# The output gate of a hybrid decoder layer: 64 column loads become 8 whole-row loads and one sum

## The chip, the cores and the metric

The kernel runs on one core of one Trainium2 chip. A core has five engines that run side by side and meet through semaphores: PE (TensorE, matrix products), DVE (VectorE), ACT (ScalarE), POOL (GpSimd) and SP (SyncE), which issues nearly all of this kernel's transfers. Each engine takes its instructions in order. The metric is the time of one execution on the device, in microseconds (us), as the median of the runs; lower is better.

## The reference, cut to what matters

One decoder layer on 1024 tokens of width 1024, all in float32. A conditioning vector `c` gives shift, scale and gate through one product; the gate is the last third of it and scales the layer's contribution to the residual stream at the very end.

```python
mod = c @ w_ada[l] + b_ada[l]                      # (1, 3072)
shift, scale, gate = jnp.split(mod, 3, axis=-1)
h = rmsnorm(x, norm_gain[l]) * (1.0 + scale[:, None, :]) + shift[:, None, :]
proj = h @ w_in[l]                                 # q, k, v, gates of both branches
...
o_a = stick_breaking_attention(...)                # 8 heads of 64
...
o_b = latent_attention(...)                        # 8 heads
...
merged = jax.nn.sigmoid(g_a) * y_a + jax.nn.sigmoid(g_b) * y_b
x = x + gate[:, None, :] * (merged @ w_out[l])
return rmsnorm(x, final_norm_gain)
```

So the gate is a vector of 1024 numbers, a product of `c` (1024) with a 1024x1024 slice of `w_ada`, needed only in the last tenth of the kernel.

## The kernel before, in words

The opening stage loads x and weights, makes h transposed (`hh` and `hl`, a rounded part and the rest, since products are made of three passes of rounded operands), and the first q, k and v. Then four pairs of stick-breaking heads follow (`sb_pair(m)`, m = 0 to 3). For each head and each of 8 query blocks i, `sb_scores` makes scores with q and k on PE (L723, L724, into `ps_s`), two sigmoids on ACT (`surv`, `beta`), a running product on DVE (the scan, L727) and the weights on POOL (L729, L730, `beta`). `finish` then turns the weights with PE (L678, into `ps_t`), takes them out as `wth` (ACT) and `wtl` (the rest, DVE), and multiplies them with v (L695, into `ps_o`) after every second block.

Beside a pair runs `filler`, a generator of projection jobs. One job loads a 512 KB column block of `w_in` (`raw`, issued by SP), splits it into `whi` (DVE) and `wlo` (mostly POOL), and makes two halves of 24 matmuls of 512 columns each (L298, into `ps_g`). The halves are taken out through `ev`, a buffer of two slots, by ACT, or as q and k of the next pair by ACT and DVE (`q1a`, `kl1b` and the like). POOL also works off a chain of small operations for the rotary tables (`rope`, tiles `rp`).

The third generator, `gates_gen`, computes the output gate. Before the change, `gate_part(n)` works on 128 of the 1024 columns at a time: for k = 0 to 7 it loads a 128x128 block of `w_ada` into `wg`, which takes a slot of `ev`, and adds block times `c` to `ga` on DVE (L794, L796). It then loads the bias (L799, L800), rounds the sum into `gr` (two tiles), sums the 128 rows with two matmuls against `ones_r` (L807), copies the row out (DVE) and stores it to `gate_d`. The loop around the pairs advances it by one step in each step of pairs 0, 1 and 2.

The order on each engine isn't that of the code. A scheduler reorders the instructions by a timeline of its own, within what the tiles' slots and data allow, so that gate steps, scans, casts and evacuations are mixed on DVE, and `wg`, `raw`, `v` and the stores on SP.

Of the kernel before, what the change touches and what calls it, by code (L numbers as in the profile page):

```python
# [10 lines left out]
F32 = mybir.dt.float32  # L11
F32R = mybir.dt.float32r
# [3 lines left out]
ALU = mybir.AluOpType  # L16
# [3 lines left out]
P = 128  # L20
S = 1024
D = 1024
NT = S // P
KD = D // P
# [19 lines left out]
def hsl(hf):  # L44
    return slice(hf * 512, (hf + 1) * 512)
# [3 lines left out]
def hybrid_layer(ctx: ExitStack, tc: tile.TileContext, x, c, positions, w_ada, b_ada, norm_gain, w_in,  # L49
                 q_norm_gain, w_uq, kv_norm_gain, w_ukv, w_branch_a, w_branch_b, w_out, final_norm_gain, out):  # L50
    nc = tc.nc
    xf, of = x[0], out[0]
    win = w_in[0].rearrange("(k p) n -> p k n", p=P)
    wada = w_ada[0].rearrange("(k p) n -> p k n", p=P)
# [18 lines left out]
    def ps_tile(tag):  # L73
        return PS["pool"].tile([P, 512], F32, tag=tag, name="ps_" + tag, bufs=PS["bufs"][tag])
# [5 lines left out]
    gate_d = dram.tile([1, D], F32, name="gate_d")  # L80
# [3 lines left out]
    def copy(eng, o, i):  # L84
        if eng == "a":
            nc.scalar.activation(o, i, AF.Copy)  # L86
        elif eng == "v":
            nc.vector.tensor_copy(out=o, in_=i)  # L88
        else:
            nc.gpsimd.tensor_scalar(out=o, in0=i, scalar1=1.0, scalar2=None, op0=ALU.mult)  # L90

    def rd(t):
        return t.bitcast(F32)

    def rest(eng, o, full, hi):
        (nc.vector if eng == "v" else nc.gpsimd).tensor_tensor(out=o, in0=full, in1=rd(hi), op=ALU.subtract)  # L96
# [219 lines left out]
    def advance(gen, n):  # L316
        for _ in range(n):
            if next(gen, "end") == "end":
                return False
        return True  # L320
# [42 lines left out]
    def load_v(m):  # L363
        st = pairs[m]
        st.v = sbp.tile([P, NT, 2, P], F32R, name=f"v{m}", tag="v", bufs=2)
        nc.sync.dma_start(out=rd(st.v), in_=v_d[:, :, m])
# [50 lines left out]
    with tc.tile_pool(name="start", bufs=1, **RW, side="right") as st:  # L417
# [167 lines left out]
        for k in range(KD):  # L585
            n = k + 1
# [74 lines left out]
    evp = evx.enter_context(tc.tile_pool(name="evp", bufs=2, **RW, side="right"))  # L661
    sbx = ExitStack()
    sbp = sbx.enter_context(tc.tile_pool(name="sbp", bufs=1, **RW, side="right"))
# [69 lines left out]
    def sb_pair(m):  # L733
        st = pairs[m]
        og = sbp.tile([P, S], F32, name=f"oga{m}", tag="og", bufs=1)
        todo = []
        for h in range(2):
            wts = {}
            for i in range(NT):
                beta = sb_scores(m, h, i)  # L740
                todo.append((h, i, beta))
                yield
                if len(todo) > 1:
                    finish(m, st, og, todo.pop(0))
                    yield
        finish(m, st, og, todo.pop(0))
        yield
        nc.sync.dma_start(out=oa_d[m], in_=og)
# [34 lines left out]
    ones_r = base.tile([P, 1], F32R, name="ones_r")  # L783
    nc.vector.tensor_copy(out=ones_r, in_=ones_c)

    def gate_part(n):
        c0 = 2 * D + n * 128
        ga = sbp.tile([P, 128], F32, name="ga", tag="ga", bufs=1)
        for k in range(KD):
            wg = evp.tile([P, 512], F32, name="wg", tag="ev")[:, 0:128]  # L790
            nc.sync.dma_start(out=wg, in_=wada[:, k, c0:c0 + 128])
            cc = col[:, R_C + k:R_C + k + 1]
            if k == 0:
                nc.vector.tensor_scalar(out=ga, in0=wg, scalar1=cc, scalar2=None, op0=ALU.mult)  # L794
            else:
                nc.vector.scalar_tensor_tensor(out=ga, in0=wg, scalar=cc, in1=ga, op0=ALU.mult, op1=ALU.add)  # L796
            yield
        wg = evp.tile([P, 512], F32, name="wg", tag="ev")[0:1, 0:128]
        nc.sync.dma_start(out=wg, in_=b_ada[:, c0:c0 + 128])  # L799
        nc.vector.tensor_tensor(out=ga[0:1], in0=ga[0:1], in1=wg, op=ALU.add)  # L800
        yield
        gr = [sbp.tile([P, 128], F32R, name=f"gr{i}", tag=f"gr{i}", bufs=1) for i in range(2)]
        copy("v", gr[0], ga)
        rest("v", gr[1], ga, gr[0])
        ps = ps_tile("g")
        for i in range(2):
            nc.tensor.matmul(out=ps[0:1, 0:128], lhsT=ones_r, rhs=gr[i], start=i == 0, stop=i == 1)  # L807
        wg = evp.tile([P, 512], F32, name="wg", tag="ev")[0:1, 0:128]
        copy("v", wg, ps[0:1, 0:128])
        nc.sync.dma_start(out=gate_d[:, n * 128:(n + 1) * 128], in_=wg)  # L810
        yield

    gates_gen = itertools.chain.from_iterable(gate_part(n) for n in range(8))
    for m in range(NPAIR):
        units = 14 if m + 1 < NPAIR else 16 - TAILF
        done = 0
        for step, _ in enumerate(sb_pair(m)):
            want = min(units, units * (step + 1) // 31)
            advance(filler, want - done)
            done = want  # L820
            if m in (1, 2):
                advance(rope, 2)
            if step == VLS and m + 1 < NPAIR:
                load_v(m + 1)
            if m < 3:
                advance(gates_gen, 1)
        advance(filler, units - done)
    advance(rope, 1000)
# [28 lines left out]
    with tc.tile_pool(name="latw", bufs=2, **RW, side="right") as lp:  # L857
# [32 lines left out]
        for t in range(NT):  # L890
# [4 lines left out]
            for k in range(KD):  # L895
                for n, (m, w) in enumerate(((hh, wch), (hh, wcl), (hl, wch))):
# [7 lines left out]
            v = small.tile([P, 2], F32, name="vl", tag="vl")  # L904
# [7 lines left out]
                                    op0=ALU.mult)  # L912
# [77 lines left out]
    for k in range(2):  # L990
        raw = up.tile([P, S], F32, name="ur", tag="ur", bufs=URB)
        nc.sync.dma_start(out=raw, in_=wukv[:, k, :])
        g = col[:, R_KG + k:R_KG + k + 1]
# [64 lines left out]
    for t in range(NT):  # L1058
        tsl = slice(t * P, (t + 1) * P)
        pq = [ps_tile("g"), ps_tile("s")]  # L1060
        for k in range(3):
            for n, (m, w) in enumerate(((cq_h, wqh), (cq_h, wql), (cq_l, wqh))):
                for b in range(2):
                    nc.tensor.matmul(out=pq[b][:, 0:384], lhsT=m[:, k, tsl], rhs=w[:, k, b * 384:(b + 1) * 384],  # L1064
                                     start=k == 0 and n == 0, stop=k == 2 and n == 2)
# [16 lines left out]
        if t > 3:  # L1082
            b, n = divmod(t - 4, 2)
# [148 lines left out]
    step, done, total = 0, 0, 2 * len(yajobs) - len(UQF) - UQE  # L1232
# [64 lines left out]
    for t in range(NT):  # L1297
# [8 lines left out]
        for n, (hf, c0, wc) in enumerate(parts):  # L1306
            hi, lo = wos[hf]
            cs, gs = slice(c0, c0 + wc), slice(hf * 512 + c0, hf * 512 + c0 + wc)
            ps = ps_tile("sgt"[n])
            for k in range(KD):  # L1310
                for i, (m, w) in enumerate(((mg[0], hi), (mg[0], lo), (mg[1], hi))):
                    nc.tensor.matmul(out=ps[:, 0:wc], lhsT=m[k][:, tsl], rhs=w[:, k, cs],  # L1312
                                     start=k == 0 and i == 0, stop=k == KD - 1 and i == 2)
# [5 lines left out]
            if n == 0:  # L1319
                nc.vector.tensor_scalar(out=acc, in0=ss[:, 0:1], scalar1=1.0 / D, scalar2=EPS, op0=ALU.mult,  # L1320
                                        op1=ALU.add)
            else:
                nc.vector.scalar_tensor_tensor(out=acc, in0=ss[:, n:n + 1], scalar=1.0 / D, in1=acc, op0=ALU.mult,
                                               op1=ALU.add)
# [31 lines left out]
```

## Time and profile before

| | |
|---|---|
| median of 3 runs | 1001.03 us (1000.28 to 1006.5) |
| profiled execution | 1001.96 us |
| its span, first to last instruction | 1000.2 us |
| busy in the span | PE 954.9 us (95%), DVE 647.6 (65%), ACT 435.5 (44%), POOL 388.5 (39%) |
| mean granted clock of PE | 0.992 of 2.4 GHz |
| gate work | from 121.9 us (first load) to 403.0 us (last store) |

A profile's busy time counts an engine as busy while an instruction is under way. Matmuls overlap, so the duration of one (0.39 us for 512 columns) is longer than the distance to the next; the distances between starts are the ones to add up. "Idle before, releaser" is the time an engine stood before an instruction, and what ended that.

### The profile page before, as it was taken

To read this page: it belongs to the slowest core of one execution; us is meant where nothing else is said; L and a number is where in the kernel's file an instruction comes from. 1 tells how busy PE (TensorE), PEld (TensorE's weight loads), DVE (VectorE), ACT (ScalarE), POOL (GpSimd) and SP (SyncE) were. 2 spreads that over 40 slices of the span, in tenths; PEclk is the share of its full clock that TensorE was granted. 3 is DMA by queue.
4 is the path that set the end of the run, shared out by engine and by line. 5 is a ranking of instruction groups with operands and counts; after the bars stand their busy time and mean duration, and the time that the engine had idled before them with its cause. 6 is when DMAs were issued, how large, how long until landed. Compare 5 with 4: busy or idle time off the path is not lost.

```text
span 1000.2 us, 14638 instructions
## 1 busy us (share of the span) xinstructions
PE 954.9 (95%) x5100; PEld 815.5 (82%) x5100; DVE 647.6 (65%) x1294; ACT 435.5 (44%) x981; POOL 388.5 (39%) x393
## 2 busy tenths in 40 slices
PE   4979998998999989999999999999999999999997
PEld 3657877887787878888888999988899998877886
DVE  4862566678568857476655454774689997586544
ACT  4363433343333443343443432543488886333211
POOL 1100399994434435345444000621103332586322
PEclk9989999999999999999999999999999999999999
DMA  9733452213322142212122500479555332884322
GB/s 292 226 114 106 150 164 76 82 35 82 117 87 77 39 141 71 65 43 85 56 82 71 156 17 1 158 261 307 186 137 148 102 96 80 269 263 157 126 85 85
DMA packets 127140, 122.40 MB, mean 122 GB/s; under 512 B 16029, under 2 KB 97050, under 8 KB 126682
## 3 DMA queue, kind: packets, MB, share of 16 engines
q1 hardware_dynamic: 127002, 121.45, 39.2%
q8 instruction: 40, 0.66, 0.3%
q14 instruction: 34, 0.28, 0.1%
q10 hardware_dynamic: 64, 0.02, 0.0%
HBM read 86.80 MB, written 34.64 MB: 121 GB/s over the span
## 4 chain that ended last, share of the span: by engine, by line
PE 74%; DVE 10%; DMA 9%; issue 3%; ACT 2%; POOL 1%; SPq 1%; DVEq 0%; POOLq 0%; ACTq 0%
PE ps_g L298 29%; PE ps_o L695 6%; PE ps_t L678 6%; PE ps_g L1312 4%; PE ps_s L1312 4%; DMA wg<-in_w_ada 4%; PE ps_g L898 3%; PE ps_s L899 3%; PE ps_s L1133 2%; PE ps_s L1135 2%; PE ps_s L1134 2%; PE ps_t L1013 2%; DVE acc L483 1%; PE ps_s L533 1%; PE ps_g L1064 1%
## 5 line engine op out<-in xcount | busy, mean ns | idle before, releaser
L298 PE MATMUL ps_g<-hh,whi 128*128 128x512 f32 x448 | 179.3, 400 | 1.5 <-DVE kl1b L96 1.5
L298 PE MATMUL ps_g<-hl,whi 128*128 128x512 f32 x448 | 177.3, 396 | 0.0
L298 PE MATMUL ps_g<-hh,wlo 128*128 128x512 f32 x448 | 176.8, 395 | 0.0
L96 POOL TENSOR_TENSOR wlo<-raw,whi 128x1024 fp32r<-128x1024 f32 (+1 forms) x45 | 92.0, 2045 | 171.5 <-DVE whi L88 107.3
L727 DVE TENSOR_TENSOR_SCAN surv<-surv,diag 128x128 f32<-128x128 f32 (+3 forms) x64 | 110.2, 1728 | 25.0 <-ACT surv L725 23.8
L96 DVE TENSOR_TENSOR wtl<-ps_t,wth 128x512 fp32r<-128x512 f32 (+1 forms) x192 | 102.4, 548 | 19.1 <-ACT wth L86 17.7
L730 POOL TENSOR_TENSOR beta<-beta,surv 128x127 f32<-128x127 f32 (+3 forms) x64 | 82.3, 1287 | 58.3 <-DVE surv L727 58.1
L86 ACT ACTIVATE wth<-ps_t 128x512 fp32r<-128x512 f32 (+1 forms) x192 | 90.5, 491 | 23.3 <-PE ps_t L678 20.7
L298 PEld LDWEIGHTS ps_g<-hh,whi 128*128 128x128 f32 x448 | 85.1, 190 | 18.0 <-issue 2.0
L298 PEld LDWEIGHTS ps_g<-hh,wlo 128*128 128x128 f32 x448 | 84.9, 189 | 17.7
L298 PEld LDWEIGHTS ps_g<-hl,whi 128*128 128x128 f32 x448 | 85.2, 190 | 15.7
L726 ACT ACTIVATE beta<-ps_s 128x512 f32<-128x512 f32 (+2 forms) x96 | 48.1, 504 | 26.8 <-POOL beta L730 26.7
L725 ACT ACTIVATE surv<-ps_s 128x512 f32<-128x512 f32 (+2 forms) x96 | 47.9, 500 | 23.5 <-POOL beta L730 8.8
L1145 ACT ACTIVATE sc<-sc,mx 128x128 f32<-128x128 f32 (+3 forms) x64 | 49.3, 771 | 15.2 <-DVE mx L1136 15.0
L88 DVE CAST whi<-raw 128x1024 fp32r<-128x1024 f32 (+1 forms) x46 | 33.2, 721 | 33.6 <-PE ps_g L298 29.0
L390 ACT ACTIVATE ev<-ps_g 128x512 f32<-128x512 f32 x32 | 19.1, 598 | 80.2 <-PE ps_g L298 56.3
L796 DVE SCALAR_TENSOR_TENSOR ga<-wg,col,ga 128x128 f32<-128x128 f32 x56 | 30.6, 546 | 34.0 <-DMA wg<-in_w_ada 33.4
L86 ACT ACTIVATE otmp<-ps_o 64x256 f32<-64x256 f32 x64 | 24.2, 378 | 50.7 <-PE ps_o L695 49.8
L678 PE MATMUL ps_t<-ident,beta 128*128 128x128 f32 x288 | 43.2, 274 | 2.4 <-POOL beta L729 1.9
L678 PE MATMUL ps_t<-ident,sc 128*128 128x128 f32 x288 | 44.9, 275 | 0.1
L707 POOL TENSOR_TENSOR oga<-oga,zs 64x256 f32<-64x256 f32 x32 | 33.0, 1031 | 28.9 <-DVE oga L705 28.1
L1312 PE MATMUL ps_s<-woh,mg 128*128 128x512 f32 x128 | 41.5, 391 | 1.2 <-ACT mg L86 1.2
(420 smaller groups left out, 2423.7 us busy)
## 6 DMA issues: line engine op xcount, KB each, us to landing
raw<-in_w_in SPq DMA_DIRECT2D x35, 512.0 KB
wa<-in_w_ada SPq DMA_DIRECT2D x32, 256.0 KB
x<-in_x SPq DMA_DIRECT2D x8, 512.0 KB
v_d<-vo SPq DMA_DIRECT2D x8, 512.0 KB
v<-v_d SPq DMA_DIRECT2D x4, 1024.0 KB
wg<-in_w_ada SPq DMA_DIRECT2D x64, 64.0 KB
ga_d<-ev SPq DMA_DIRECT2D x16, 256.0 KB
gb_d<-ev SPq DMA_DIRECT2D x16, 256.0 KB
```

Of the source, the lines that this page charges most:

```text
L86: nc.scalar.activation(o, i, AF.Copy)
L88: nc.vector.tensor_copy(out=o, in_=i)
L96: (nc.vector if eng == "v" else nc.gpsimd).tensor_tensor(out=o, in0=full, in1=rd(hi), op=ALU.subtract)
L298: nc.tensor.matmul(out=ps, lhsT=w[:, k, :], rhs=m[k][:, hsl(hf)], start=n == 0, stop=n == last)
L678: anchor[0] = nc.tensor.transpose(out=pt[:, b * P:(b + 1) * P], in_=w[:, (j0 + b) * P:(j0 + b + 1) * P], identity=ident)
L695: anchor[0] = nc.tensor.matmul(out=po[:, qs], lhsT=vtile(j), rhs=wts[j // 4][n][:, j % 4, qs], start=j == 0 and n == 0, stop=j == i and n ...
L725: nc.scalar.activation(surv[:, c0:c0 + wc], ps[:, 0:wc], AF.Sigmoid, scale=-0.125)
L726: nc.scalar.activation(beta[:, c0:c0 + wc], ps[:, 0:wc], AF.Sigmoid, scale=0.125)
L727: nc.vector.tensor_tensor_scan(out=surv[:, 0:w][:, ::-1], data0=surv[:, 0:w][:, ::-1], data1=diag1[:, S - w:S][:, ::-1], initial=0.0, op0= ...
L730: nc.gpsimd.tensor_tensor(out=beta[:, 0:w - 1], in0=beta[:, 0:w - 1], in1=surv[:, 1:w], op=ALU.mult)
L1145: nc.scalar.activation(sc[:, 0:w], sc[:, 0:w], AF.Exp, bias=mx[:, len(chunks) - 1:len(chunks)] if CH else mx[:, 0:1], scale=-1.0, accum_ou ...
L1312: nc.tensor.matmul(out=ps[:, 0:wc], lhsT=m[k][:, tsl], rhs=w[:, k, cs], start=k == 0 and i == 0, stop=k == KD - 1 and i == 2)
```

## The change

The gate is computed in one go. `gate_sum` loads whole rows: 8 loads of 128x1024 into a buffer `wg` of two slots of its own, and 16 steps on DVE, two halves of 512 columns for each load, add up one tile `gsum`. The bias is one load of 1024 columns and one addition. The sum is rounded once into two tiles `gr`, which take the slots of `wg`, and the rows are summed at the end by two matmuls for each half. A step of the generator is now asked for in every fourth step of all four pairs.

```diff
-    def gate_part(n):
-        c0 = 2 * D + n * 128
-        ga = sbp.tile([P, 128], F32, name="ga", tag="ga", bufs=1)
+    gsum = sbp.tile([P, D], F32, name="gsum")
+
+    def gate_sum():
+        wgs = {}
+
+        def load_g(k):
+            wgs[k] = sbp.tile([P, D], F32, name="wg", tag="wg", bufs=2)
+            nc.sync.dma_start(out=wgs[k], in_=wada[:, k, 2 * D:3 * D])
+
+        load_g(0)
+        load_g(1)
+        yield
         for k in range(KD):
-            wg = evp.tile([P, 512], F32, name="wg", tag="ev")[:, 0:128]
-            nc.sync.dma_start(out=wg, in_=wada[:, k, c0:c0 + 128])
             cc = col[:, R_C + k:R_C + k + 1]
...
+            for hf in range(2):
+                o, i = gsum[:, hsl(hf)], wgs[k][:, hsl(hf)]
+                if k == 0:
+                    nc.vector.tensor_scalar(out=o, in0=i, scalar1=cc, scalar2=None, op0=ALU.mult)
+                else:
+                    nc.vector.scalar_tensor_tensor(out=o, in0=i, scalar=cc, in1=o, op0=ALU.mult, op1=ALU.add)
+                if hf == 1 and k + 2 < KD:
+                    load_g(k + 2)
+                yield
+        bg = sbp.tile([P, D], F32, name="bg", tag="wg", bufs=2)[0:1]
+        nc.sync.dma_start(out=bg, in_=b_ada[:, 2 * D:3 * D])
+        yield
+        nc.vector.tensor_tensor(out=gsum[0:1], in0=gsum[0:1], in1=bg, op=ALU.add)
+        yield
+        gr = [sbp.tile([P, D], F32R, name=f"gr{i}", tag="wg", bufs=2) for i in range(2)]
+        for hf in range(2):
+            copy("v", gr[0][:, hsl(hf)], gsum[:, hsl(hf)])
+            rest("v", gr[1][:, hsl(hf)], gsum[:, hsl(hf)], gr[0][:, hsl(hf)])
             yield
...
+        for hf in range(2):
+            ps = ps_tile("g")
+            for i in range(2):
+                nc.tensor.matmul(out=ps[0:1], lhsT=ones_r, rhs=gr[i][:, hsl(hf)], start=i == 0, stop=i == 1)
+            row = evp.tile([P, 512], F32, name="grow", tag="ev")[0:1]
+            copy("v", row, ps[0:1])
+            nc.sync.dma_start(out=gate_d[:, hsl(hf)], in_=row)
+            yield
...
-            if m < 3:
+            if step % 4 == 3:
                 advance(gates_gen, 1)
```

What the scheduler makes of it shows in the order of the instructions. On DVE, in pair 0 around query blocks 3 to 5 of its first head, this stood before (a scan of 128x512 is block 3's, one of 128x768 block 5's; `wtl` 128x4x128 is block 3's part of the turned weights):

```order
L727 SCALAR_TENSOR_TENSOR surv<-surv,diag_974 128x512
L96 TENSOR_TENSOR wtl<-ps_t,wth 128x2x128
L727 SCALAR_TENSOR_TENSOR surv<-surv,diag_974 128x640
L96 TENSOR_TENSOR wtl<-ps_t,wth 128x3x128
L705 TENSOR_TENSOR oga_1049<-ps_o,otmp 64x256
L796 SCALAR_TENSOR_TENSOR ga<-wg,col,ga 128x128
L96 TENSOR_TENSOR wtl<-ps_t,wth 128x4x128
L796 SCALAR_TENSOR_TENSOR ga<-wg,col,ga 128x128
L88 CAST whi<-raw 128x1024
L800 TENSOR_TENSOR ga<-ga,wg 1x128
L88 CAST gr_1320<-ga 128x128
L727 SCALAR_TENSOR_TENSOR surv<-surv,diag_974 128x768
```

The same place on DVE now:

```order
L96 TENSOR_TENSOR wtl<-ps_t,wth 128x2x128
L727 SCALAR_TENSOR_TENSOR surv<-surv,diag_974 128x640
L805 SCALAR_TENSOR_TENSOR gsum<-wg,col,gsum 128x512 x4
L96 TENSOR_TENSOR wtl<-ps_t,wth 128x3x128
L705 TENSOR_TENSOR oga_1050<-ps_o,otmp 64x256
L805 SCALAR_TENSOR_TENSOR gsum<-wg,col,gsum 128x512 x4
L812 TENSOR_TENSOR gsum<-gsum,bg 1x1024
L96 TENSOR_TENSOR wtl<-ps_t,wth 128x4x128
L88 CAST whi<-raw 128x1024
L88 CAST gr_3594<-gsum 128x512 x2
L96 TENSOR_TENSOR gr_3595<-gsum,gr_3594 128x512 x2
L727 SCALAR_TENSOR_TENSOR surv<-surv,diag_974 128x768
```

Eight of the sixteen steps, the bias and the rounding stand in this piece; the other eight (two first steps, six more) stand before it, in pairs, between the casts of k of pair 0 and the scan of block 3. Behind it DVE has two row copies of the gate and nothing else of it.

On PE, the same pair, the products of block 3's weights with v stood like this before, with the first gate matmul right behind:

```order
L695 MATMUL ps_o<-wth,v_1045 128x256
L723 MATMUL ps_s<-k0a,q0a 128x512
L724 MATMUL ps_s<-kl0a,q0a 128x512
L695 MATMUL ps_o<-wtl,v_1045 128x256
L695 MATMUL ps_o<-wth,v_1045 128x256
L695 MATMUL ps_o<-wtl,v_1045 128x256
L695 MATMUL ps_o<-wth,v_1045 128x256
L695 MATMUL ps_o<-wtl,v_1045 128x256
L695 MATMUL ps_o<-wth,v_1045 128x128
L695 MATMUL ps_o<-wtl,v_1045 128x128
L678 MATMUL ps_t<-ident,beta 128x128
L723 MATMUL ps_s<-k0a,q0a 128x384
```

And on PE now:

```order
L298 MATMUL ps_g<-hh_113,whi 128x512
L695 MATMUL ps_o<-wth,v_1045 128x256
L298 MATMUL ps_g<-hl_121,whi 128x512
L298 MATMUL ps_g<-hh_113,wlo 128x512
L298 MATMUL ps_g<-hh_114,whi 128x512
L298 MATMUL ps_g<-hl_122,whi 128x512
L298 MATMUL ps_g<-hh_114,wlo 128x512
L298 MATMUL ps_g<-hh_115,whi 128x512
L298 MATMUL ps_g<-hl_123,whi 128x512
L298 MATMUL ps_g<-hh_115,wlo 128x512
L695 MATMUL ps_o<-wtl,v_1045 128x256
L695 MATMUL ps_o<-wth,v_1045 128x256
```

Eight projection matmuls, and four more ahead of the first row of `wth`, moved in front of the first use of block 3's `wtl`. The gate's own matmuls on PE stand in pair 2 now, two for each half, the first half here:

```order
L723 MATMUL ps_s<-k2b,q2b 128x128
L724 MATMUL ps_s<-kl2b,q2b 128x128
L822 MATMUL ps_g<-gr_3594,ones_r 1x512
L822 MATMUL ps_g<-gr_3595,ones_r 1x512
L678 MATMUL ps_t<-ident,beta 128x128 x4
```

Before, sixteen of them (L807) were spread over pairs 0 to 2, a few instructions behind the rounding of their `gr`.

## Rows read from the trace of the kernel before

**Rows 1.** Busy time by stretch: us, PE, PEld, DVE, ACT, POOL, granted clock, DMA share, GB/s.

```profile
122.00:222.00 100.00, 95.90 (x479) 80.13 (x478) 69.68 (x101) 37.26 (x87) 93.05 (x132) 0.98 0.32 96
222.00:322.00 100.00, 93.76 (x492) 78.41 (x491) 70.91 (x100) 37.85 (x88) 43.91 (x49) 1.00 0.30 91
322.00:422.00 100.00, 96.40 (x492) 80.67 (x491) 65.46 (x92) 37.09 (x85) 40.15 (x42) 0.98 0.26 79
422.00:560.00 138.00, 137.55 (x726) 117.18 (x725) 82.52 (x100) 59.98 (x133) 62.01 (x61) 1.00 0.24 72
```

**Rows 2.** Waits of PE, 122 to 422 us: us in total, times, longest.

```profile
PE ps_g L807 <- DVE gr L88: 7.3, 3, 3.0
PE ps_o L695 <- DVE wtl L96: 2.6, 3, 1.3
PE ps_t L678 <- POOL beta L729: 1.9, 1, 1.9
PE ps_g L298 <- DVE kl1b L96: 1.5, 1, 1.5
PE ps_t L678 <- DVE wtl L96: 0.5, 1, 0.5
```

**Rows 3.** Tile wg: duration ns min/median/max; then engine idle until (us, times).

```profile
L796 DVE SCALAR_TENSOR_TENSOR ga<-wg,col,ga x56: 320/352/2959, 130.4 to 398.5; 128x128 f32<-128x128 f32 x56
...
  DMA wg<-in_w_ada: 36.0, 26
```

**Rows 4.** Stretches of 1 us behind two of the waits, columns as in rows 1.

```profile
159.00:160.00 1.00, 1.00 (x4) 0.81 (x3) 1.00 (x3) 0.00 (x0) 1.00 (x3) 0.50 1.07 318
367.00:368.00 1.00, 1.00 (x4) 0.81 (x3) 0.00 (x0) 0.00 (x0) 0.99 (x1) 0.50 0.00 0
```

**Rows 5.** PE in order of time: start, us, instruction, idle before it and releaser.

```profile
153.51 0.28 PE L695 MATMUL ps_o<-wtl,v 128*128 128x256 f32 x1
...
157.80 0.27 PE L807 MATMUL ps_g<-gr,ones_r 128*1 128x128 f32 x1 [2.87 <-DVE gr L88]
...
161.22 0.39 PE L298 MATMUL ps_g<-hh,wlo 128*128 128x512 f32 x1
161.45 0.39 PE L298 MATMUL ps_g<-hh,whi 128*128 128x512 f32 x1
...
364.49 0.22 PE L807 MATMUL ps_g<-gr,ones_r 128*1 128x128 f32 x1 [3.01 <-DVE gr L88]
```

**Rows 6.** The chain that ended last, 340 to 370 us: start, us, what.

```profile
358.75 4.02 DMA oa_d<-oga
```

**Rows 7.** Groups by form on DVE: busy us, mean ns, idle before and releaser.

```profile
L796 DVE SCALAR_TENSOR_TENSOR ga<-wg,col,ga 128x128 f32<-128x128 f32 x56 | 30.6, 546 | 34.0 <-DMA wg<-in_w_ada 33.4
```

**Rows 8.** Tiles acc and raw on DVE: ns min/median/max, first and last start, form.

```profile
L483 DVE SCALAR_TENSOR_TENSOR acc<-wa,col,acc x50: 473/485/689, 6.4 to 64.0; 128x256 f32<-128x256 f32 x50
...
L854 DVE SCALAR_TENSOR_TENSOR wql<-raw,col,wqh x3: 1017/1017/1020, 573.2 to 578.1; 128x768 fp32r<-128x768 f32 x3
L96 DVE TENSOR_TENSOR wlo<-raw,whi x1: 1228/1228/1228, 109.8 to 109.8; 128x1024 fp32r<-128x1024 f32 x1
```

**Rows 9.** DVE in order of time, columns as in rows 5.

```profile
128.38 0.33 DVE L794 TENSOR_SCALAR ga<-wg,col 128x128 f32<-128x128 f32 x1 [2.54 <-DMA wg<-in_w_ada]
...
149.65 0.69 DVE L96 TENSOR_TENSOR wtl<-ps_t,wth 128x512 fp32r<-128x512 f32 x1 [0.29 <-ACT wth L86]
...
237.12 0.35 DVE L796 SCALAR_TENSOR_TENSOR ga<-wg,col,ga 128x128 f32<-128x128 f32 x1 [1.57 <-DMA wg<-in_w_ada]
```

**Rows 10.** The instructions on tile ga alone, 128 to 150 us: DVE busy, clock, DMA.

```profile
128.00:150.00 22.00, 3.29 (x7) 1.00 0.48 141
```

**Rows 11.** Waits of DVE, 128 to 150 us: us in total, times, longest.

```profile
DVE ga L796 <- DMA wg<-in_w_ada: 3.7, 3, 1.4
DVE ga L794 <- DMA wg<-in_w_ada: 2.5, 1, 2.5
DVE wtl L96 <- ACT wth L86: 2.4, 2, 2.1
```

More of the change, by code (lines that the diff above doesn't have):

```diff
@@ L792, in gate_part @@
             cc = col[:, R_C + k:R_C + k + 1]
[L793 to L796, printed above, removed]
-            yield
-        wg = evp.tile([P, 512], F32, name="wg", tag="ev")[0:1, 0:128]
-        nc.sync.dma_start(out=wg, in_=b_ada[:, c0:c0 + 128])
-        nc.vector.tensor_tensor(out=ga[0:1], in0=ga[0:1], in1=wg, op=ALU.add)
@@ L801, in gate_part @@
[L801 to L810, printed above, removed]
@@ L811, in gate_part @@
-        yield
-    gates_gen = itertools.chain.from_iterable(gate_part(n) for n in range(8))
+            for hf in range(2):
[7 more added lines that the diff above has]
+                yield
@@ L814, in hybrid_layer @@
+        for hf in range(2):
[6 more added lines that the diff above has]
+            yield
+    gates_gen = gate_sum()
     for m in range(NPAIR):
```

## Prediction

> **What bounds the kernel now.** I began with the stretches, because the change lives in one part of the program: 122 to 422 us, in which pairs 0 to 2 of the stick-breaking branch run beside the gate sum. The 138 us after it (the end of pair 2 and pair 3) have the same kind of work, evacuations of q and k included, but no gate work, and serve as a yardstick. TensorE (PE) is busy for 95.90, 93.76 and 96.40 of each 100 us, and for 137.55 of 138 in the yardstick [rows 1]. So PE sets the pace, and an edit on VectorE (DVE) or on the DMA queue is worth what it gives back of PE's gaps, nothing more. The gaps are 4.1 + 6.2 + 3.6 = 13.9 us. The list of what PE waited for in the same 300 us names 13.8 us of them [rows 2]: 7.3 us in three waits on `gr`, the rounded gate sum (L807), 2.6 us in three on `wtl` (the DVE half of the transposed weights), 1.9 us on POOL's `beta`, 1.5 us on `kl1b`, 0.5 us on `wtl` once more. DVE is far from full (about 70 of 100), but it runs in order and stands 36.0 us, 26 times, at loads of `wg` [rows 3].
>
> A wait of PE also has an aftermath. Behind the 2.87 us wait that ends at 157.80, the granted clock reads 0.50 [rows 4], the lower of the two levels (1.2 instead of 2.4 GHz): from there to 161.22 eight L298 matmuls start, 0.43 us apart, and the next one comes after 0.23 us [rows 5]. Eight at 0.23 are 1.8 us instead of 3.4, so this costs 1.5 us. The 3.01 us wait that ends at 364.49 [rows 5] is followed by the same level [rows 4]; I charge 1.5 us again. The second stretch has waits of 1.9 us and less, and its clock reads 1.00 [rows 1, 2]. In all the gate's stretch loses 13.8 + 3.0 = **16.8 us**, and this is the most that the change could win.
>
> **The change part by part.**
>
> *Loads.* 64 loads of 64 KB become 8 of 512 KB; the bytes are the same 4 MB. The two slots `ev`, which the gate shared with ACT's evacuations, are rid of them. PE's list has no wait of L298 on ACT, so I give nothing for that. A 512 KB transfer with 4 KB rows is in the trace as the store `oa_d`, 4.02 us from issue to landing [rows 6], and I take that for a load. Only two slots turn over (bufs=2), so load k+2 is issued after both steps that read load k.
>
> *DVE work.* Now 56 steps of 128 columns take 30.6 us, 546 ns in the mean, with a median of 352 [rows 3, 7]; with first steps, bias, rounding and copies there are 96 gate instructions. New: a 128x256 step takes 485 ns and a 128x768 step 1,017 [rows 8], so 512 columns lie at 0.75 us on the line between them, 16 steps at 12.0 us. The bias row has one partition and 1,024 columns; the length counts, so I take the 1.23 us of a 128x1024 subtraction [rows 8]. That is 13.2 us to the end of the bias. Rounding, rest and the two row copies are six more of 512 columns, under 0.7 us each by the `wtl` of that width [rows 9]: 4 us. So DVE does 17 us instead of 30.6 and more, and its standing of 36 us shrinks to that at eight loads. By itself that is worth nothing; what PE waits for is.
>
> *Where the order puts it.* The scheduler pulls all 16 steps, the bias and the rounding into the first third of pair 0, ahead of the scan of block 5 (128x768). After that DVE has no gate work but two row copies. The matmuls with `ones_r` go to pair 2, two pairs behind `gr`. So the three waits on `gr` go, 7.3 us with both clock drops: **10.3 us**, at no price in PE work (16 matmuls of 128 columns become 4 of 512). What is late next is other work of the DVE queue, and there the gate steps are gone too. Ahead of the wait on `kl1b`, DVE stood 1.57 us at a wg load that ended at 237.12, just before it turned to that crowd of casts [rows 9]. I take the 2.6 + 1.5 + 0.5 = **4.6 us** on `wtl` and `kl1b` as gone, since the yardstick has the same evacuations and gaps of 0.45 us in all. I keep the **1.9 us** on `beta`: POOL is busy for 93 of the first 100 us [rows 1] with the rotary tables, which stay. If it goes too, that is the upper end.
>
> *The burst in pair 0.* This is the cost. I replayed DVE up to the `wtl` of block 3 (128x512), which PE takes at 153.51 [rows 5]. In the trace DVE waits 2.54 us for the first load, until 128.38, and finishes that `wtl` at 149.65 + 0.69 = 150.34 [rows 9]. Since 125.84 that is 24.5 us: 3.3 us of gate steps [rows 10], 6.2 us at wg loads, 2.4 us at ACT [rows 11], and 12.6 us of other work. New: 12.6 + 13.2 = 25.8 us, which ends at 151.6 without any wait. The waits, worked from 4.02 us for a load: the first has eight times the bytes of the old one, so 3.5 us instead of 2.5; load 2 is asked for while v's second megabyte is still under way, 0 to 2 us; load 6 is issued after the steps on load 4, and DVE reaches it after two steps (1.5 us) and two short operations (1 us), so 1.5 us show; the bias load follows load 6 in the same way, 0 to 1 us. Together 5 to 8 us: ready between 156.6 and 159.6. PE comes later too, since 12 L298 matmuls (2.8 us at 0.23) now stand ahead of that use: 156.3. The wait is 0.3 to 3.3 us; I take **1.5 us**, near the low end, as ACT is freed from the wg slots. If the mean excess over the median, 194 ns, falls on all 14 two-input steps, 2.7 us more, it is 6.0 us, and with a clock drop 7.5: the upper bound.
>
> *A new order of everything else.* PE's rows between 122 and 440 us are shuffled; behind that the sequence is the same. The yardstick, 0.45 us in 138, gives 1.0 us for 300. The other end is 4.6 us, as much as the other queues' waits make up now. I take **1.0 us**, by the yardstick, since the same scheduler ordered it.
>
> **Sum.** 16.8 - 1.9 - 1.5 - 1.0 = 12.4 us won. The profiled execution took 1001.96 us (span 1000.2), so 989.6 us; the median of the runs is 0.9 us lower than it. I forecast **989.5 us**. With the upper ends, 7.5 and 4.6, 2.8 us remain, 999.2 us; with nothing kept and nothing new 985.2.
>
> **Rivals.**
>
> *A, half the gain (994 to 1000 us).* The first pair doesn't give its time back, because POOL holds it. For it: POOL has 7 us of slack in the first 100 us [rows 1], and 2.87 + 1.5 us of the loss to be removed lie there. If those 4.4 stay as waits on POOL and the burst adds 2 us, 12.4 - 4.4 - 2 = 6 us, 996. Against it: of PE's waits only the 1.9 us are on POOL.
>
> *B, slower.* Each of the 14 long steps has two inputs in SBUF and runs while POOL is all but full. The worst step in the trace took 2,959 ns instead of 320 [rows 3], 2.64 us more. If half of the 14 met that, DVE would be 18 us later, PE would stand nearly as long at the block 3 `wtl`, and a clock drop would follow: 989.6 + 18 + 1.5 = 1009. Slower than before begins at 12 us of lengthening. The rows speak against it: the mean excess is 0.19 us, over 56 steps in three pairs.
>
> The Trainium skill speaks for B ("SBUF — State Buffer", section "Who interferes with whom"): a DVE instruction with two SBUF inputs and a GpSimd instruction that reads SBUF exclude each other, and whichever issues first holds the shared ports for its whole length. The trace agrees in kind, with a median of 352 ns beside a worst of 2,959. By that rule the step's own length doesn't matter, only how often it meets POOL, and 14 meetings for 56 would be a gain.
>
> *C, all of it goes (under 986 us).* DVE is so relieved that POOL, which waits for its scans, runs ahead too. For it: the yardstick. Against it: the rotary tables.
>
> *D, nothing moves.* Were the gate hidden anyway, other waits would end last at the same places. Against it stand the `gr` waits: the next L298 matmuls started right behind them [rows 5].
>
> **How the numbers follow.** The forecast, 986 to 994 us, has 0.55; A 0.25; C 0.10; B and D 0.05 each. A measurement of this kernel can tell about 1% from no change, so faster means under 991.0: seven tenths of the forecast's share, and C, together 0.49. Slower is B, 0.05. The rest, 0.46, is within 1%. The range, 984 to 1000 us, holds the forecast, A and most of C.
>
> **What would show it.** Right: the matmuls with `ones_r` have no wait of PE; from 170 us on DVE waits for no gate load and the granted clock stays at 1.00; PE's gaps in the three stretches fall to some 4, 1 and 0.5 us. The burst shows as 14 steps of 0.75 us between 129 and 160 us, and as a wait of PE on `wtl` near 156. Wrong: steps of 2 us and more in the burst (B), a gate load that takes far longer than 4 us behind what SP has queued, or new gaps on `beta` and `wlo` with POOL full (A).

## The result, and the profile after

The changed kernel takes 0.9942 of the time of the kernel before (95% interval 0.9928 to 0.9957): medians of 998.7 and 1004.9 us over 15 runs each, so 0.6% faster, some 5.8 us. 12.4 us were forecast. In what follows, "x us under before" is one minus the ratio, times the median of before in the same comparison (1003.6 to 1004.9 us); the profiled execution of the changed kernel took 999.91 us.

Busy time by stretch, after, columns as in [rows 1]:

```profile
122.00:222.00 100.00, 90.75 (x433) 75.02 (x433) 65.24 (x81) 33.75 (x79) 92.31 (x123) 0.95 0.40 122
222.00:322.00 100.00, 100.00 (x520) 84.84 (x519) 57.63 (x68) 40.38 (x92) 52.76 (x57) 1.00 0.25 74
322.00:422.00 100.00, 100.00 (x522) 85.00 (x522) 60.45 (x73) 42.28 (x98) 45.98 (x47) 1.00 0.24 72
422.00:560.00 138.00, 137.55 (x722) 116.98 (x722) 81.72 (x100) 59.24 (x128) 58.35 (x58) 1.00 0.25 74
```

The gaps of the second and third hundred are gone (6.2 and 3.6 us before, now nothing). Those of the first more than doubled, from 4.1 to 9.3 us. The list of PE's waits in the 300 us, which answers to [rows 2], names other things than before:

```profile
PE ps_o L695 <- DVE wtl L96: 4.1, 2, 2.3
PE ps_t L678 <- POOL beta L730: 4.0, 2, 2.5
PE ps_o L695 <- ACT wth L86: 1.2, 1, 1.2
```

No wait on `gr` is left; the matmuls with `ones_r` start at 417 and 432 us as part of the stream. But there are two long waits on `wtl` and, 10 and 18 us behind the second of them, waits on POOL and ACT; one more on POOL stands at 219 us. PE in order of time shows where:

```profile
146.84 0.39 PE L695 MATMUL ps_o<-wtl,v 128*128 128x256 f32 x1 [1.81 <-DVE wtl L96]
...
149.28 0.63 PE L298 MATMUL ps_g<-hh,wlo 128*128 128x512 f32 x1
149.71 0.63 PE L298 MATMUL ps_g<-hh,whi 128*128 128x512 f32 x1
...
158.38 0.39 PE L298 MATMUL ps_g<-hh,wlo 128*128 128x512 f32 x1
161.04 0.56 PE L695 MATMUL ps_o<-wtl,v 128*128 128x256 f32 x1 [2.27 <-DVE wtl L96]
...
171.14 0.88 PE L678 MATMUL ps_t<-ident,beta 128*128 128x128 f32 x6 [1.50 <-POOL beta L730]
178.90 0.39 PE L695 MATMUL ps_o<-wth,v 128*128 128x256 f32 x1 [1.17 <-ACT wth L86]
...
218.91 1.17 PE L678 MATMUL ps_t<-ident,beta 128*128 128x128 f32 x5 [2.48 <-POOL beta L730]
```

In the old order the first of these uses, that of block 1's `wtl`, had waited half as long:

```profile
144.69 0.39 PE L695 MATMUL ps_o<-wtl,v 128*128 128x256 f32 x1 [0.90 <-DVE wtl L96]
```

Behind the first wait the projection matmuls start 0.43 us apart instead of 0.23. The granted clock says the same, in stretches of 1 us: it is at its lower level of 1.2 GHz after three of these waits.

```profile
148.00:149.00 1.00, 1.00 (x4) 0.81 (x3) 1.00 (x2) 0.00 (x0) 1.00 (x1) 0.50 0.70 208
...
162.00:163.00 1.00, 1.00 (x7) 1.00 (x6) 1.00 (x3) 0.19 (x1) 1.00 (x1) 0.50 0.00 0
...
220.00:221.00 1.00, 1.00 (x4) 0.81 (x3) 0.46 (x1) 0.67 (x2) 0.91 (x2) 0.50 0.00 0
```

What kept `wtl` away is the row of gate steps on DVE, with the loads that it waits for, and in front of block 1's `wtl` also a scan of 3.42 us. The view of the tile `gsum` gives their durations, DVE in order of time their place, 141 to 165 us:

```profile
L805 DVE SCALAR_TENSOR_TENSOR gsum<-wg,col,gsum x14: 742/936/1799, 132.9 to 158.1; 128x512 f32<-128x512 f32 x14
...
L812 DVE TENSOR_TENSOR gsum<-gsum,bg x1: 1354/1354/1354, 159.0 to 159.0; 1x1024 f32<-1x1024 f32 x1
its engine sat idle before it (us, times) until:
  DMA wg<-in_w_ada: 4.9, 4
```

```profile
143.06 3.42 DVE L727 TENSOR_TENSOR_SCAN surv<-surv,diag 128x512 f32<-128x512 f32 x1
...
148.25 4.63 DVE L805 SCALAR_TENSOR_TENSOR gsum<-wg,col,gsum 128x512 f32<-128x512 f32 x4
...
157.20 1.79 DVE L805 SCALAR_TENSOR_TENSOR gsum<-wg,col,gsum 128x512 f32<-128x512 f32 x2 [1.47 <-DMA wg<-in_w_ada]
159.03 1.35 DVE L812 TENSOR_TENSOR gsum<-gsum,bg 1x1024 f32<-1x1024 f32 x1
160.31 0.67 DVE L96 TENSOR_TENSOR wtl<-ps_t,wth 128x512 fp32r<-128x512 f32 x1
...
163.39 1.74 DVE L727 TENSOR_TENSOR_SCAN surv<-surv,diag 128x768 f32<-128x768 f32 x1
```

The `wtl` of block 3 ends at 160.98, and PE had been ready for it since 158.77. What follows runs over DVE and POOL. DVE's next scan, block 5's, starts only at 163.39, behind the steps, the bias, this `wtl` and the rounding of `gr`; the sigmoids that it reads were done at 156.21:

```profile
155.82 0.39 ACT L725 ACTIVATE surv<-ps_s 128x256 f32<-128x256 f32 x1
```

Beside the rounding and this scan, POOL's `wlo` runs:

```profile
161.72 5.61 POOL L96 TENSOR_TENSOR wlo<-raw,whi 128x1024 fp32r<-128x1024 f32 x1 [0.73 <-issue]
167.30 2.24 POOL L151 TENSOR_SCALAR rp<-rp 128x128 f32<-128x128 f32 x1
...
169.54 1.54 POOL L730 TENSOR_TENSOR beta<-beta,surv 128x767 f32<-128x767 f32 x1
```

It took 5.61 us (the median of this operation is 2.39), the table step behind it 2.24 instead of 0.54, and the `beta` that PE waits for at 171.14 stands behind both. The late `wth` of 178.90 hangs on POOL too, since ACT made it behind an operation that had waited for a `beta`:

```profile
177.27 1.08 ACT L726 ACTIVATE beta<-ps_s 128x512 f32<-128x512 f32 x2 [5.07 <-POOL beta L730]
```

The gain in the profile's own time is smaller than in the medians. The last score matmul of pair 3 (L723 on `q3b`) starts at 530.7 us instead of 535.8, but what lies behind it, in the same order in both kernels, took 467.4 us in this execution instead of 464.4. In the profiles of all the kernels here it took between these two times, so this difference isn't the change's.

### The profile page after: what moved, and what is told of

Same layout as the page of the kernel before. It is cut to its first block, busy times and chain, and to the rows that moved or that the text cites. A ratio compares the mean times of both kernels' runs of the same rounds, so it can differ in the third digit from the quotient of the medians.

```text
span 998.1 us, 14364 instructions
## 1 busy us (share of the span) xinstructions
PE 955.7 (96%) x5088; PEld 816.4 (82%) x5088; DVE 620.3 (62%) x1221; ACT 435.6 (44%) x981; POOL 398.6 (40%) x393
## 4 chain that ended last, share of the span: by engine, by line
PE 73%; DMA 7%; DVE 7%; POOL 6%; issue 3%; ACT 2%; SPq 1%; DVEq 0%; POOLq 0%; ACTq 0%
PE ps_g L298 29%; PE ps_o L695 6%; PE ps_t L678 6%; PE ps_g L1327 4%; PE ps_s L1327 3%; PE ps_g L913 3%; PE ps_s L914 3%; POOL rp L151 2%; DMA ya_d<-gl 2%; PE ps_s L1148 2%; PE ps_s L1149 2%; PE ps_s L1150 2%; PE ps_s L724 1%; POOL wlo L96 1%; PE ps_s L723 1%
## 5 line engine op out<-in xcount | busy, mean ns | idle before, releaser
L96 POOL TENSOR_TENSOR wlo<-raw,whi 128x1024 fp32r<-128x1024 f32 (+1 forms) x45 | 95.5, 2123 | 183.6 <-DVE whi L88 114.9
L1333 POOL TENSOR_TENSOR xr<-xr,fgain 128x512 f32<-128x512 f32 (+1 forms) x17 | 20.7, 1222 | 57.5 <-ACT yr L1332 56.6
L695 PE MATMUL ps_o<-wtl,v 128*128 128x256 f32 (+1 forms) x160 | 38.9, 289 | 4.5 <-DVE wtl L96 4.5
```

The costliest lines, as they stand in the source:

```text
L695: anchor[0] = nc.tensor.matmul(out=po[:, qs], lhsT=vtile(j), rhs=wts[j // 4][n][:, j % 4, qs], start=j == 0 and n == 0, stop=j == i and n ...
```

## The experiments

**Theory** after the result: the burst of 16 steps in the first third of pair 0 gives back half of what the waits on `gr` and the fragments cost. **Rivals:** POOL, with the rotary tables, holds pair 0 whatever the gate does; or the new order of the other work costs the time.

### No gate, spread steps, short steps, tables moved

**nogate** leaves the gate's product out; the bias row alone goes to `gate_d`.

```diff
-    gsum = sbp.tile([P, D], F32, name="gsum")
...
+        bg = sbp.tile([P, D], F32, name="bg")[0:1]
+        nc.sync.dma_start(out=bg, in_=b_ada[:, 2 * D:3 * D])
+        yield
+        nc.sync.dma_start(out=gate_d[:, :], in_=bg)
```

> Leaves the gate's product out: the bias row alone goes to gate_d. It is the bound of what any treatment of the gate can win. Theory 1 (the burst of 16 steps on DVE in pair 0 gives back half the gain): without steps PE's gaps from 122 to 222 us fall from 9.3 us to under 2, and the time is 14 to 17 us under before (ratio 0.983 to 0.986). Theory 2 (POOL holds pair 0, with or without the gate): gaps of 5 us and more on beta stay in pair 0, and the time is 6 to 10 us under before (0.990 to 0.994). Theory 3 (the new order of the other work costs it): gaps stay in pair 0 and new ones stand elsewhere, 6 to 10 us under before too, on wtl and kl rather than on beta.

Measured: ratio 0.9862 (0.9843 to 0.9882), 13.9 us under before, just short of the first theory's 14 to 17. So this is all that the gate could give back in this order, not 16.8. Its waits of PE, 122 to 560 us:

```profile
PE ps_t L678 <- POOL beta L730: 7.0, 4, 4.6
PE ps_o L695 <- DVE wtl L96: 0.4, 1, 0.4
```

With no gate at all, PE waits 7.0 us on POOL's `beta`, 4.6 of them at 226 us, where the tables end. Both theories have a part: the waits on `wtl` are the gate's, and `beta` is waited for without the gate too.

**held** ties the DVE instructions of each gate step behind the DVE instruction at its place in the code, so that the 16 steps lie spread, from 144 us in pair 0 to 350 us in pair 2.

```diff
+    def newest(eng):
+        return next(i for i in reversed(list(nc.cur_bb.bb.instructions)) if i.engine == eng.engine)
...
             if step % 4 == 3:
-                advance(gates_gen, 1)
+                with tc.issue_after(newest(nc.vector)):
+                    advance(gates_gen, 1)
```

> The changed kernel with each gate step held behind the DVE instruction at its place in the code, so that the 16 steps are spread over pairs 0 to 3. All the same work and loads. Theory 1 (the burst): the waits on wtl near 147 and 161 us and what follows them to 180 us go, PE's gaps from 122 to 222 us are 2 to 4 us, and the time is 12 to 15 us under before (0.985 to 0.988). Theory 2 (POOL): beta waits of 4 us stay in pair 0, and it is as the changed kernel, 5 to 7 us under before (0.993 to 0.995).

Measured: 0.9906 (0.9887 to 0.9925), 9.4 us under before, between the two. The burst's waits are gone, but its list of waits names 7.9 us on `beta` and, new, 2.8 us on the row copy, which was tied down as well:

```profile
PE ps_g L298 <- DVE grow L88: 2.8, 1, 2.8
```

**onein** leaves out the running sum: each step is a product with one input in SBUF.

```diff
-                if k == 0:
-                    nc.vector.tensor_scalar(out=o, in0=i, scalar1=cc, scalar2=None, op0=ALU.mult)
-                else:
-                    nc.vector.scalar_tensor_tensor(out=o, in0=i, scalar=cc, in1=o, op0=ALU.mult, op1=ALU.add)
+                nc.vector.tensor_scalar(out=o, in0=i, scalar1=cc, scalar2=None, op0=ALU.mult)
```

> The changed kernel with the running sum left out: each of the 16 steps is a product with one input in SBUF, so the sum is not formed; order, loads and number of steps stay. The first two steps of this form took 0.50 us beside 1.07 in the mean for the 14 others. Theory 1 with the length of the burst: 14 steps are 8 us shorter, the wait on wtl near 161 us goes, and with it what follows; 10 to 13 us under before (0.987 to 0.990). Theory 1 with the loads: the burst is bound by the eight loads one behind another, DVE waits for them as long as the steps were, and the time stays within 2 us of the changed kernel. Theory 2 (POOL): also within 2 us of the changed kernel.

Measured: 0.9902 (0.9879 to 0.9925), 9.8 us under before, just short of the range for the burst's length. The steps took 0.57 us in the median, and block 3's `wtl` was done at 154.8 us. But the scheduler had moved PE's use of it too, to 152.7, so that a wait of 2.13 us stands there all the same, and `wtl` still holds 4.1 us in all. (Of both shifts 1.7 us are an opening stage that ended earlier in this profile.) The run says that shorter steps help; it doesn't separate the burst's length from its place.

**ropeheld** ties the tables to their place in the code, pairs 1 and 2 (the scheduler had pulled them into pair 0).

```diff
             if m in (1, 2):
-                advance(rope, 2)
+                with tc.issue_after(newest(nc.gpsimd)):
+                    advance(rope, 2)
```

> The changed kernel with the rotary tables' POOL work held at its place in the code, in pairs 1 and 2, so that POOL is half empty in pair 0 while the burst stays there. Theory 2 (POOL): the beta waits and the late wth in pair 0 go and steps fall to 0.75 us each, so the burst ends 4 us earlier: 9 to 13 us under before (0.987 to 0.991). Theory 1 with loads or order alone: the wait on wtl near 161 us stays at 1.5 us or more, the steps are shorter but the time is 5 to 8 us under before (0.992 to 0.995). If POOL's work is needed in time in pairs 1 and 2, new waits on beta there, and no gain.

Measured: 0.9970 (0.9958 to 0.9982), 3.0 us under before and worse than the changed kernel. POOL only moved its crowd, now into pair 1, as the third expectation said:

```profile
PE ps_t L678 <- POOL beta L730: 11.4, 8, 3.7
```

The largest of these, 3.7 us at 166 us, stands in pair 0, where POOL had nothing of the tables any more. There `wlo` took 5.60 us again, beside the same rounding and scan on DVE:

```profile
157.59 5.60 POOL L96 TENSOR_TENSOR wlo<-raw,whi 128x1024 fp32r<-128x1024 f32 x1 [6.00 <-issue]
```

So the burst can make a wait on POOL as well.

### Rounding held, steps held, tables spread

**roundheld** leaves the steps where they were and holds back the four rounding instructions to pair 2.

```diff
-            if step % 4 == 3:
+            if step % 4 == 3 and nh[0] < 18:
+                nh[0] += 1
                 advance(gates_gen, 1)
+            if m == 2 and step == 3:
+                advance(gates_gen, 1)
+            if m == 2 and step in (11, 15):
+                with tc.issue_after(newest(nc.vector)):
+                    advance(gates_gen, 1)
```

> The changed kernel with the bias and the 16 steps where they were, but the four rounding instructions of gr held back to the middle of pair 2. Theory 1a (the steps delay wtl, and the rounding behind them keeps POOL out: its wlo took 5.6 us instead of 2.4 beside it, and beta came late): the waits on wtl near 147 and 161 us stay (3 to 4 us), wlo there takes 2.4 us, the waits on beta and wth of 5.2 us from 168 to 180 us go; 8 to 11 us under before (0.989 to 0.992), 3 to 5 better than the changed kernel. Theory 1b (beta is late only because the steps made everything late): the beta waits stay at 4 us or more; 5 to 7 us under before (0.993 to 0.995).

Measured: 0.9938 (0.9919 to 0.9958), 6.2 us under before, as the changed kernel. `wlo` took 2.39 us there and the first wait on `beta` shrank from 1.50 to 0.16 us, but `beta` still holds 6.0 us in all and `wtl` 4.2. So the rounding alone isn't what costs the time. What such a collision costs this run doesn't isolate, since in its place another POOL operation stood still, a table step (median 0.54 us), beside the bias addition, two subtractions, a cast and the scan:

```profile
158.87 4.21 POOL L151 TENSOR_SCALAR rp<-rp 128x128 f32<-128x128 f32 x1
```

**held2** is held with matmuls and row copies left free.

```diff
-            if step % 4 == 3:
-                advance(gates_gen, 1)
+            if step % 4 == 3 and nh[0] < 21:
+                nh[0] += 1
+                with tc.issue_after(newest(nc.vector)):
+                    advance(gates_gen, 1)
```

> As the kernel with the steps held at their places, but the matmuls with ones_r and the row copies are left free, so that the 2.8 us wait of PE on the row copy near 430 us goes. The burst is gone, the load on POOL in pair 0 isn't. Expected by theory 1 with POOL next: waits of 5 to 8 us on beta in all, at 190 to 230 us, nothing on wtl or grow over 0.6 us; 10 to 13 us under before (0.987 to 0.990). By theory 1 alone (POOL costs nothing once the burst is gone): 14 us and more under before.

Measured: 0.9875 (0.9858 to 0.9892), 12.6 us under before, as expected with POOL next. The steps took 0.75 us in the median instead of 0.94, no engine waited for a load of `wg`, and of PE's waits from 122 to 560 us one line is left:

```profile
PE ps_t L678 <- POOL beta L730: 7.9, 5, 3.3
```

**held2_ropespread** spreads the tables too: one step of them is asked for in every second step of a pair, and POOL is done with them at 353 us, early in pair 2.

```diff
-            if m in (1, 2):
-                advance(rope, 2)
+            if step % 2 == 1:
+                with tc.issue_after(newest(nc.gpsimd)):
+                    advance(rope, 1)
```

> The same, with the rotary tables' POOL work spread evenly over pairs 0 to 3 instead of all in pair 0. Theory of two limits (burst on DVE, POOL next): the beta waits of 5 to 8 us go too, PE's gaps from 122 to 422 us are under 2.5 us in all and the granted clock stays at 1.00; 15 to 18 us under before (0.982 to 0.985). Theory 1 alone: as without the spreading, within 2 us. If POOL only moves its crowd: new beta waits in pairs 1 to 3 of 3 us and more, and 10 to 13 us under before.

Measured: 983.76 us, ratio 0.9795 (0.9779 to 0.9811), 20.6 us under before, more than expected. It is the best kernel of the study that computes the gate. PE stands 0.9 us in 300, and POOL is at 66, 71 and 60 of each 100 us instead of 93, 44 and 40 [rows 1]:

```profile
122.00:222.00 100.00, 100.00 (x514) 84.90 (x513) 62.46 (x77) 41.63 (x96) 66.00 (x82) 1.00 0.37 111
222.00:322.00 100.00, 100.00 (x518) 84.92 (x517) 69.82 (x80) 41.20 (x95) 71.13 (x85) 1.00 0.30 90
322.00:422.00 100.00, 99.07 (x518) 83.89 (x517) 69.33 (x76) 40.25 (x93) 59.66 (x72) 1.00 0.24 72
```

**nogate_ropespread** is nogate with the same three lines.

> The gate's product left out (the bias row alone goes to gate_d), with the rotary tables' work spread over pairs 0 to 3. Without the gate and without the crowd on POOL nothing is left that PE waits for between 122 and 560 us: gaps under 1.5 us in all, 17 to 20 us under before (0.980 to 0.983), and 3 to 6 us under the kernel without gate whose tables stand in pair 0. If POOL was not what ended last there, it is within 1 us of that kernel (0.986).

Measured: 0.9780 (0.9764 to 0.9796), 22.1 us under before, more than the 17 to 20 expected; one line of waits is left, 0.7 us on `wtl`. With held steps and spread tables the gate costs no more than the two intervals can tell.

### One part alone, slots undone, tables spread alone

**sum_once** is the kernel before with its small loads and shared slots, but one sum, rounded and summed over the rows at the end.

```diff
-        ga = sbp.tile([P, 128], F32, name="ga", tag="ga", bufs=1)
+        ga = gsum[:, n * 128:(n + 1) * 128]
...
-        for i in range(2):
-            nc.tensor.matmul(out=ps[0:1, 0:128], lhsT=ones_r, rhs=gr[i], start=i == 0, stop=i == 1)
+    gates_gen = itertools.chain(itertools.chain.from_iterable(gate_part(n) for n in range(8)), gate_rows())
```

> The kernel before with one part of the change alone: its 64 small loads and 64 steps of 128 columns stay in the slots they share with ACT, but they fill one sum, which is rounded and summed over the rows once at the end. Theory (waits on gr were worth 10.3 us, POOL takes some of it): the waits on gr go, beta waits grow from 1.9 to 5 us as in the kernel without gate; 4 to 7 us under before (0.993 to 0.996). Rival (the fragments of DVE work and the loads of wg are what holds PE, wherever the rows are summed): other waits on wtl and kl take the place of those on gr, within 2 us of before. If nothing took their place: 9 to 11 us under (0.989 to 0.991).

Measured: 0.9930 (0.9909 to 0.9950), 7.0 us under before, the upper end of the range. The waits on `gr` are gone. What took their place was not `beta` (0.8 us) but `wtl`, the rival's line:

```profile
PE ps_o L695 <- DVE wtl L96: 8.8, 5, 3.3
```

So this part alone gives as much as the whole change.

**shared** undoes the slots: 16 loads of 128x512, each in a slot of `ev`.

```diff
-            wgs[k] = sbp.tile([P, D], F32, name="wg", tag="wg", bufs=2)
-            nc.sync.dma_start(out=wgs[k], in_=wada[:, k, 2 * D:3 * D])
...
+                i = evp.tile([P, 512], F32, name="wg", tag="ev")
+                nc.sync.dma_start(out=i, in_=wada[:, k, 2 * D + hf * 512:2 * D + (hf + 1) * 512])
```

> The changed kernel with the slots undone: 16 loads of 128x512, each in a slot of ev as before, so that the loads take turns with ACT's evacuations; steps, sum, rounding and rows as changed, nothing held by hand. Theory (slots of their own let the scheduler pull all steps into pair 0): the shared slots spread the steps over pairs 0 to 2, the waits on wtl near 147 and 161 us go, beta waits of 5 to 8 us stay; 8 to 13 us under before (0.987 to 0.992), better than the changed kernel. Rival (sharing costs as much as the burst, since evacuations wait for loads and PE for evacuations): 4 to 7 us under before, as the changed kernel.

Measured: 0.9880 (0.9855 to 0.9905), 12.0 us under before, inside the range. In its order on DVE the steps lie in ones to threes from the first scan of pair 0 to the eleventh of pair 1, with nothing held by hand. PE's waits, 122 to 560 us, have no `wtl` of the burst:

```profile
PE ps_t L678 <- POOL beta L730: 5.7, 4, 2.6
PE ps_o L695 <- DVE wtl L96: 0.5, 1, 0.5
```

Sharing, then, was a brake that kept the scheduler from pulling the steps together. This run also halves the loads; that their size had no part in it was not tested alone.

**after_ropespread** and **before_ropespread** are the two kernels with the three lines of held2_ropespread.

> The changed kernel, burst and all, with the rotary tables' POOL work spread over pairs 0 to 3. If the two limits add up: the waits on wtl near 147 and 161 us stay at 2 to 4 us, those on beta behind them fall to 2 us or less; 12 to 16 us under before (0.984 to 0.988). If the burst only hurts because POOL is full: the waits on wtl go as well, and it comes within 2 us of the kernel with held steps and spread tables (0.979 to 0.982). If the burst alone sets pair 0: 6 to 9 us under before.

> The kernel before, gate and all, with the rotary tables' POOL work spread over pairs 0 to 3. If POOL was hidden behind the gate's waits, as the rows before say (1.9 us on beta): 0 to 4 us under before (0.996 to 1.000), and the change is worth 10 us and more on top of the spreading. If POOL's crowd made the waits on gr and wtl too, through DVE: 6 to 10 us under before (0.990 to 0.994).

Measured: 0.9886 (0.9862 to 0.9911), 11.4 us under before, below the range for a plain sum of the two; and 0.9983 (0.9968 to 0.9997), 1.7 us, inside its range. In the first, a wait of 4.0 us on `beta` is left at 168 us behind a `wlo` of 5.59 us, and 3.2 us on `wtl`. So on top of spread tables the change is worth 9.7 us, just short of the 10 expected. The eight kernels make a table, as ratios to before:

| | tables in pair 0 | tables spread |
|---|---|---|
| before | 1 | 0.9983 |
| changed, with its burst | 0.9942 | 0.9886 |
| changed, steps held (held2) | 0.9875 | 0.9795 |
| no gate | 0.9862 | 0.9780 |

Each ratio is to runs of the kernel before on the same chip; the rows were not all run on one. Down a column, the burst costs 6.7 us with the tables in pair 0 and 9.1 with the tables spread (0.0067 and 0.0091 of 1004 us). Along a row, the crowd on POOL costs 1.7 us while the gate's waits cover it, 5.6 beside the burst, and 8.0 and 8.2 once both are gone. For the third theory, that the new order itself costs, no run has a sign: the order was rebuilt in each of these kernels, and the best lose next to nothing. The profiles place the gains in the pairs: from the first score matmul of pair 0 to the last of pair 3 it is 407.2 us before, 402.3 with the change, 396.3 in held2, 396.2 in nogate, 387.1 in held2_ropespread and 386.0 in nogate_ropespread.

## Why the prediction was wrong

The direction was right and the size not quite half of it: 5.8 us instead of 12.4. The time lies inside the range and where rival A put it. It missed the 989.5 us by 9.2, more than the gain did, because before takes 1004.9 us in the median of 15 runs and not the 1001.03 of the first three.

- **The step that failed is the burst in pair 0**, "I take 1.5 us, near the low end". By held2 it costs 6.7. The wait that I replayed came out at 2.27 us, inside the 0.3 to 3.3, with luck: DVE was to have block 3's `wtl` ready between 156.6 and 159.6 and had it at 160.98, PE was to come at 156.3 and came at 158.77, and the two delays nearly cancel. And that was one wait of four. I looked at the use of block 3 only. Block 1's `wtl` already stood behind two of the steps and a scan of 3.42 us: 1.81 us. The lost time went on through DVE's next scan and POOL: 1.50 and 1.17 us. And the clock fell twice; one minus the granted clock, summed over the microseconds from 147 to 151 and 161 to 165, is 1.7 us each. That is 10.2 us in this profile, where the old order had lost 5.5 in the same place (0.90 us on `wtl` at 144.69, and 2.87 on `gr` with a drop of 1.7 by the same sum). The forecast had 6.6 us too much in all; this term was too small by 6.7 - 1.5 = 5.2, and beside spread tables the burst costs even 9.1.
- **The 1.9 us kept on `beta`** were too small as well. Without a gate `beta` holds 7.0 us, with held steps 7.9. The gate's waits had covered most of what POOL's tables cost; I read a wait of the old profile as what would be left of it. By the table the crowd costs 5.6 us beside the burst and 8.0 with the steps held. In the changed kernel it shows as the 2.48 us at 218.91, with a clock drop behind it; most of it was still hidden, now behind the burst.
- **The 16.8 us as the most** that the change could win fell too: without the gate and with the tables where they are it is 13.9 us, and with both out of the way 22.1. The two terms above were too small by more than the 6.6 us together; the forecast missed by no more because the 16.8, too, were 5.3 too few, which is luck. The list of waits doesn't hold all that PE lost: in the pairs its busy time fell from 393.3 us before to 385.8 in nogate_ropespread, and the two clock drops are some 3.4 of these 7.5 us. What the rest is, no run says.
- **Right: the waits on `gr`.** They went, at no price on PE. sum_once agrees with the term: 7.0 us, where 10.3 were charged and `wtl` took a part back.
- **Right: `wtl` and `kl1b` behind pair 0.** PE has no gap from 222 to 422 us, so the 3.3 of the 4.6 us that had stood there went; the other 1.2 had stood in pair 0, where the burst put longer ones. The new order of the rest shows no price of its own: 0.45 us from 422 to 560 us as before, 0.9 in 300 in the best kernel.
- **Right: the DVE work**, 18.1 us in 21 instructions on `gsum`, rounding included, and 1.3 us for the two row copies, for 17 forecast, though a long step took 0.99 us of busy time in the mean (13.88 us for 14) instead of 0.75. The loads took 4.7 to 8.9 us, not 4.02, and DVE stood 4.9 us at them, where 5 to 8 were reckoned.
- **Rival A** had the number and half the mechanism: POOL takes a share, but pair 0 was lost on `wtl` first. **Rival B** had the mechanism of the long steps: with POOL full they took 0.94 us in the median, and 0.75 both spread out (held2) and packed with the tables gone from pair 0 (after_ropespread). It was no 18 us. The clock didn't stay at 1.00 from 170 us on, as the sign for being right had it; it fell once more behind the wait of 2.48 us at 218.91.

## What to carry to other kernels

Slots that a stage shares with other work can also be a brake on the scheduler. When you give the stage slots of its own, look in the new order for where its steps pile up, and price every use behind the pile, on every engine of the chain, not just one of them. The wait that a profile shows on an engine is what the others leave uncovered; a run with the stage left out tells what would come next before the forecast is summed. Where two loads crowd one stretch, spread both: here neither alone (12.6 and 11.4 us) gave two thirds of the 20.6 us that both gave.

## What the runs showed of the hardware

A row of DVE instructions can hold up a POOL instruction for longer than any one of them lasts. A table step took 4.21 us instead of 0.54 beside five DVE instructions in a row, of which the longest had 1.74 us. And `wlo` took 5.59 to 5.61 us in three kernels instead of 2.39, each time beside two casts, two subtractions and a scan. The Trainium skill ("SBUF — State Buffer", section "Who interferes with whom") tells of a lock that one instruction holds for its length; the runs agree with such a lock, and show that several instructions in a row can make a POOL instruction 3.7 us longer. In the other direction a scan of 128x512 took 3.42 us beside a `wlo` on POOL, where the eight of that size, this one among them, took 2.16 in the mean and the shortest 1.21.

A wait of PE of 1.81 us was followed by the lower clock level in the changed kernel, one of 1.85 us before was not (the granted clock of its stretch is 1.00 [rows 1]). Nor was one of 2.50 us in held2, here with the stretch behind it (columns as in [rows 1]):

```profile
210.37 0.77 PE L678 MATMUL ps_t<-ident,beta 128*128 128x128 f32 x5 [2.50 <-POOL beta L730]
```

```profile
211.00:212.00 1.00, 1.00 (x7) 0.82 (x6) 0.30 (x1) 0.77 (x2) 0.90 (x2) 1.00 0.00 0
```

So the length of a wait alone doesn't say whether the clock falls, and I had charged drops only behind waits of 2.9 us and more.
